# Sample attention of the second head pair beside the gates, its branch product at the end in full float32

## The chip, the core and the metric

The program runs on one core of a Trainium2 chip. The metric is the device time of one execution in microseconds (us), lower is better. Three runs of the kernel before gave 2956.97, 2960.16 and 2966.39 us; their median is 2960.16 us.

## What is computed

The reference is one layer of a hybrid decoder. It runs over 2048 prompt tokens and over 8 x 4 = 32 sample tokens, each with its own window of cached keys and values. Cut to what matters here:

```python
h = rms_norm(x, norm_pre_mix)
q, k, v, z1, z2, g_a, g_b = project_inputs(h, w_in, b_gate)     # gates: sigmoid(p + b_gate)
for gi, (win, dil) in enumerate(((128, 1), (512, 4), (2048, 16))):
    o, lse = dilated_group_prompt(...) or dilated_group_sample(...)   # 4 heads of 64 in each group
o_a = merge_dilations(outs, lses)                               # softmax over the three groups, 256 wide
o_b = z1 * (tril(w_spatial) @ layer_norm(z2) + b_spatial)       # 512 wide
merged = g_a * (o_a @ w_ao) + g_b * (o_b @ w_bo)                # 1024 wide
x = x + rms_norm(merged @ w_out, norm_post_mix)
x = x + rms_norm(square(relu(rms_norm(x, norm_pre_ffn) @ w_up)) @ w_down, norm_post_ffn)
```

For a sample token the attention of a group has 129 keys: rows of the cache at the group's dilation and the new rows of its own sequence. Everything is float32.

## The kernel before

The prompt is done in two halves of 1024 tokens (s = 0 and s = 1). The 32 sample tokens ride with the first half as columns 1024 to 1055 of every activation tile, so the first half has 1056 columns, in three chunks of 352. Each half goes through five stages: attention of the first pair of heads (hp = 0) over three groups, attention of the second pair (hp = 1), `gmlp`, `mix`, `out_rows`. After both halves comes the feed-forward part (`ffn`).

Most matrix products are done in a reduced float32 format (F32R) from split operands: a value is held as a high and a low part, and each product is three matmuls (high by high, high by low, low by high). `load_w` fetches a weight block over the SP queue (`raw`, two buffers), casts the high part on ScalarE (L264) and forms the low part on GpSimd (L267); `wh` and `wl` have two buffers each.

`mix` works on eight blocks of 128 channels. For each block it makes six gate products (two gates, three chunks, 8 K-tiles each, L283), applies the sigmoid on ScalarE (L1009), and then for each chunk makes the attention branch product `pa` (2 K-tiles from `oa`) and the gMLP branch product `pb` (4 K-tiles). VectorE multiplies the gates by them straight from PSUM (L1017 and L1019) and GpSimd adds the two (L1020). PSUM tiles of kind "g" have three buffers, of kind "s" two.

Work that is not a large product is written as Python generators in four lanes. A large product calls `tick` at certain K-tiles, and each tick takes one step of the first generator of each lane. That sets the order in which the program is written; a scheduling pass then sets the order on each engine's queue. Each engine runs its own queue strictly in order, and SP's queue issues nearly all transfers in order too.

`sample_attention(hp)` is one such generator, in lane 2. It does the attention of the sample tokens on VectorE, since the keys differ for each sequence: the 128 partitions hold 8 sequences by 16 key slots, and 30 steps take 4 keys' rows each. The score pass (L835 and L836, a product and a reduction for each of 30 steps) is followed by a softmax (L840 to L862, with two transposes on TensorE at L850 and L857), then the value pass (30 products L866, 14 pair sums L875 on VectorE, sums into `U` on GpSimd L876 and L878). Then one TensorE matmul sums over partitions (L882) and L894 transposes the result back into columns 1024 to 1055 of `oa`. The cache rows arrive in pieces of 256 KB (L807, L814, L817) in three buffers; one buffer holds the queries (L832).

Before, the generator of each head pair is pushed when that pair's first group has been projected, so that of hp = 1 runs beside the attention of hp = 1 and beside the first half of `gmlp`. There `drain(2)` makes it end before z1's second block is projected, since its buffers lie in `ov`, where z1 goes. `mix` drains lanes 0 to 2 in each block. The softmax merge of the three groups for the prompt tokens (`merge`, L751 to L766) runs at the same time in lane 1. `out_rows` multiplies by `w_out`; its own lane-2 work, `pre_mix_behind`, normalises the second half's inputs.

Of the kernel before, what the change touches and what calls it, by code (L numbers as in the profile page):

```python
# [10 lines left out]
F32 = mybir.dt.float32  # L11
# [7 lines left out]
P = 128  # L19
# [75 lines left out]
def hybrid_step(ctx: ExitStack, tc: tile.TileContext, ins: dict, outs: list):  # L95
# [176 lines left out]
    def gemm(w, offs, rhs, n, ticks=SLOW):  # L272

        calls[0] += len(offs) * n
        if calls[0] > SUM_EVERY:
            calls[0] -= SUM_EVERY
            step(3)
        pt = bank("g")
        last = len(offs) - 1
        for i, o in enumerate(offs):  # L280
            xh, xl = rhs(i)
            for j, (a, b) in enumerate(((w[0], xh), (w[0], xl), (w[1], xh))):
                nc.tensor.matmul(  # L283
                    pt[:, :n], a[:, o : o + P], b, start=(i == 0 and j == 0), stop=(i == last and j == 2)
                )
            tick(ticks.get(i, ()))
        return pt[:, :n]
# [489 lines left out]

    def sample_attention(hp):
        a0 = sm.tile([P, D], F32, tag="x", name="xt")
        a1 = sm.tile([P, D], F32, tag="x", name="xt")  # L780
        b0 = ov[:, A_X : A_X + 2048]
        q = a0[:, 0:512]
        U = a0[:, 512:1024]
        sc = a1[:, 0:240]
        pieces = [a1[:, 512:1024], b0[:, 0:512], b0[:, 512:1024]]
        prods = [b0[:, 1024:1536], b0[:, 1536:2048]]
# [100 lines left out]
        ot = sm.tile([8, 512], F32, tag="e0", name="sot")  # L887
# [9 lines left out]
        split(oh, ol, src, nc.vector)  # L897

# [94 lines left out]
    def mix(s):  # L993
        order = [4, 5, 6, 7, 0, 1, 2, 3]
        for m in range(8):
# [3 lines left out]
            gts = []  # L999
            for c, (c0, n) in enumerate(chunks(s)):  # L1000
                if c < 2:
                    gt = sm.tile([P, D], F32, tag="x", name="xt")
                else:
                    gt = sm.tile([P, D], F32, tag="t", bufs=1, name="junk")
                gts.append((gt[:, :512], gt[:, 512:]))
            for i, w in enumerate((wa, wb)):
                for c, (c0, n) in enumerate(chunks(s)):
                    pt = gemm(w, K8, act_rhs(c0, n), n)
                    nc.scalar.activation(  # L1009
                        gts[c][i][:, :n], pt, AF.Sigmoid, bias=b_gate[:, i * 8 + m : i * 8 + m + 1]  # L1010
                    )
            for lane in range(3):
                drain(lane)
            wo = load_w([w_ao[:, :, cs], w_bo[:, :, cs]])
            for (c0, n), (ga, gb) in zip(chunks(s), gts):
                pa = gemm(wo, K8[:2], lambda k: (oa[:, k, 0, c0 : c0 + n], oa[:, k, 1, c0 : c0 + n]), n)
                nc.vector.tensor_tensor(ga[:, :n], ga[:, :n], pa, ALU.mult)  # L1017
                pb = gemm(wo, K8[2:6], lambda k: (pair(k)[:, 0, c0 : c0 + n], pair(k)[:, 1, c0 : c0 + n]), n)
                nc.vector.tensor_tensor(gb[:, :n], gb[:, :n], pb, ALU.mult)  # L1019
                nc.gpsimd.tensor_tensor(row(order[m])[:, c0 : c0 + n], ga[:, :n], gb[:, :n], ALU.add)  # L1020
        for c0, n in chunks(s):
            for m in range(8):
                cc = slice(c0, c0 + n)
                split(act[:, m, 0, cc], act[:, m, 1, cc], row(order[m])[:, cc], nc.vector)

# [16 lines left out]
    def out_rows(s, behind=None):  # L1042
# [6 lines left out]
        if s == 0:  # L1049
            gain_next = gain_rows("norm_pre_mix", "t")  # L1050
            new_slot(3, False)
# [54 lines left out]
        if s == 0:  # L1106
            pt = gemm_rows([(list(zip(lhs(8), pa)), 256)], NSMP)
# [4 lines left out]
        if s == 0:  # L1112
            push(2, pre_mix_behind(1, gain_next, free))
# [400 lines left out]
    for s in range(2):  # L1514
# [6 lines left out]
        for hp in range(2):  # L1521
            for g in range(3):
# [66 lines left out]
```

## Time and profile before

| | |
|---|---|
| median of three runs | 2960.16 us |
| profiled execution, its own time | 2963.02 us |
| span of that execution in the trace | 2961.3 us |
| TensorE (PE) busy | 2849.7 us, 96% |
| VectorE (DVE) busy | 1307.1 us, 44% |
| ScalarE (ACT) busy | 1237.2 us, 42% |
| GpSimd (POOL) busy | 1192.5 us, 40% |

The 1.7 us between span and time lie outside the trace. The page cuts the span into 40 slices of 74 us and gives each engine's busy tenths in a digit. PEclk is TensorE's granted clock in tenths; it has two levels, 1.2 and 2.4 GHz, and a value between them is a mean over time at either. In a timeline row the bracket at the end says how long the engine stood idle before it and what ended the wait. In the first half, hp = 1 runs from about 296 us, `gmlp` reaches to about 497 us, the gates of `mix` follow, and `out_rows` starts at 758.8 us.

### The profile page before, as it was taken

The numbers are of one execution on the slowest core, as the hardware profiler recorded it, in microseconds if no ns is written. First come the engines' busy times: TensorE is split into PE (matmuls) and PEld (weight loads), VectorE is DVE, ScalarE is ACT, GpSimd is POOL, SyncE is SP. The second block draws the span as 40 slices with busy tenths as digits, with TensorE's granted clock in tenths as the row PEclk, the third lists the DMA queues.
The fourth block names the chain that finished last, engine by engine and source line by source line (L and its number), as shares of the span: only waits on it lengthen the run. The fifth ranks groups of instructions, "written<-read, shape, count | busy, mean of one in ns | idle before, by whom it ended". The sixth has DMA issues, their size and how long they took to land.

```text
span 2961.3 us, 44976 instructions
## 1 busy us (share of the span) xinstructions
PE 2849.7 (96%) x17350; PEld 2585.7 (87%) x17350; DVE 1307.1 (44%) x2284; ACT 1237.2 (42%) x2437; POOL 1192.5 (40%) x883
## 2 busy tenths in 40 slices
PE   7997998999998999999999999999999999999997
PEld 7897998999987887878889899999999888878885
DVE  5668687110463435450023654443333644452323
ACT  5353334212553433541135544554344555554343
POOL 3226234333312223143331344445555744445555
PEclk9998999999999999999999999999999999999998
DMA  5745654434459354253635887576665765586654
GB/s 164 189 117 158 192 145 132 111 96 109 143 177 238 122 146 116 80 135 83 150 92 198 297 270 246 181 247 207 201 205 192 238 206 185 192 275 191 191 182 149
DMA packets 463543, 514.45 MB, mean 174 GB/s; under 512 B 25440, under 2 KB 359840, under 8 KB 454112
## 3 DMA queue, kind: packets, MB, share of 16 engines
q1 hardware_dynamic: 452240, 474.54, 50.3%
q0 software_dynamic: 10944, 36.97, 6.9%
q8 instruction: 137, 2.24, 0.3%
q14 instruction: 78, 0.64, 0.1%
q10 hardware_dynamic: 144, 0.07, 0.0%
HBM read 395.92 MB, written 182.68 MB: 195 GB/s over the span
## 4 chain that ended last, share of the span: by engine, by line
PE 76%; DMA 10%; DVE 8%; POOL 2%; issue 2%; ACT 1%; SPq 0%; DVEq 0%; POOLq 0%; ACTq 0%
PE pg L283 25%; PE pd L1288 19%; PE pe L1288 10%; PE pe L1368 10%; PE pg L297 6%; DMA xt<-h 2%; PE pu L694 2%; DMA junk<-us 2%; DMA h<-h 1%; DMA us<-ov 1%; PE pt L680 1%; DMA hd<-xt 1%; DVE ov L835 1%; DMA xt<-smp 1%; DVE xt L866 1%
## 5 line engine op out<-in xcount | busy, mean ns | idle before, releaser
L283 PE MATMUL pg<-act,wh 128*128 128x352 f32 (+3 forms) x3424 | 951.4, 356 | 8.5 <-ACT ov L989 4.9
L1199 POOL TENSOR_TENSOR wf<-raw,wf 128x512 fp32r<-128x512 f32 x448 | 635.1, 1420 | 686.2 <-ACT wf L1198 630.7
L283 PEld LDWEIGHTS pg<-act,wh 128*128 128x128 f32 x3424 | 620.5, 192 | 61.3 <-ACT ov L989 5.2
L283 PE MATMUL pg<-act,wl 128*128 128x352 f32 (+3 forms) x1712 | 607.2, 355 | 0.0
L1198 ACT CAST wf<-raw 128x512 fp32r<-128x512 f32 x448 | 277.2, 619 | 502.0 <-PE pd L1288 190.7
L267 POOL TENSOR_TENSOR wl<-raw,wh 128x1024 fp32r<-128x1024 f32 (+1 forms) x106 | 254.5, 2402 | 360.8 <-ACT wh L264 337.1
L1288 PE MATMUL pd<-act,wf 128*128 128x264 f32 x2880 | 361.9, 285 | 8.6 <-ACT act L1198 5.2
L1288 PEld LDWEIGHTS pd<-act,wf 128*128 128x128 f32 x2880 | 355.2, 189 | 9.8 <-ACT act L1198 5.4
L283 PEld LDWEIGHTS pg<-act,wl 128*128 128x128 f32 x1712 | 328.4, 192 | 26.8
L1368 PE MATMUL pe<-wf,act 128*128 128x512 f32 x1008 | 237.6, 396 | 4.8 <-POOL wf L1199 4.1
L1368 PEld LDWEIGHTS pe<-wf,act 128*128 128x128 f32 x1008 | 190.2, 189 | 50.9 <-POOL wf L1199 5.4
L264 ACT CAST wh<-raw 128x1024 fp32r<-128x1024 f32 (+1 forms) x104 | 105.3, 1012 | 254.0 <-PE pg L283 141.6
L1297 DVE TENSOR_TENSOR ov<-pd,ov 128x528 f32<-128x528 f32 x140 | 96.2, 704 | 204.8 <-PE pd L1288 204.3
L1288 PE MATMUL pd<-pair,wf 128*128 128x264 f32 x1440 | 184.7, 284 | 0.0
L1288 PE MATMUL pe<-act,wf 128*128 128x512 f32 x768 | 182.6, 392 | 0.1
L1288 PEld LDWEIGHTS pd<-pair,wf 128*128 128x128 f32 x1440 | 178.2, 188 | 0.0
L1199 DVE TENSOR_TENSOR act<-flat,act 128x1024 fp32r<-128x1024 f32 (+1 forms) x76 | 103.1, 1359 | 157.4 <-ACT act L1198 157.2
L1288 PEld LDWEIGHTS pe<-act,wf 128*128 128x128 f32 x768 | 143.8, 188 | 32.9 <-ACT pair L1198 0.3
L652 ACT ACTIVATE ov<-ov 128x256 f32<-128x256 f32 (+1 forms) x192 | 91.8, 478 | 186.7 <-DVE ov L648 185.4
L1017 DVE TENSOR_TENSOR xt<-xt,pg 128x352 f32<-128x352 f32 (+1 forms) x32 | 19.3, 604 | 300.8 <-PE pg L283 164.0
L1297 DVE TENSOR_TENSOR ov<-pe,ov 128x512 f32<-128x512 f32 x136 | 91.5, 687 | 137.2 <-PE pe L1288 126.3
L1288 PE MATMUL pd<-oa,wf 128*128 128x264 f32 x1056 | 135.0, 284 | 0.0
(254 smaller groups left out, 4263.8 us busy)
## 6 DMA issues: line engine op xcount, KB each, us to landing
raw<-in_w_in_dram SPq DMA_DIRECT2D x84, 512.0 KB
raw<-up_sums SPq DMA_DIRECT2D x128, 256.0 KB
raw<-down_sums SPq DMA_DIRECT2D x128, 256.0 KB
flat<-f SPq DMA_DIRECT2D x48, 528.0 KB
raw<-in_w_up_dram SPq DMA_DIRECT2D x96, 256.0 KB
raw<-in_w_down_dram SPq DMA_DIRECT2D x96, 256.0 KB
flat<-f SPq DMA_DIRECT2D x48, 512.0 KB
f<-ov SPq DMA_DIRECT2D x16, 1056.0 KB
```

The lines of the kernel that those rows point to most:

```text
L264: nc.scalar.copy(wh[:, :o], raw[:, :o])
L267: eng.tensor_tensor(wl[:, :o], raw[:, :o], wh[:, :o].bitcast(F32), ALU.subtract)
L283: nc.tensor.matmul(pt[:, :n], a[:, o : o + P], b, start=(i == 0 and j == 0), stop=(i == last and j == 2))
L297: nc.tensor.matmul(pt[:n, o : o + width], a, b, start=(i == 0 and j == 0), stop=(i == last and j == 2))
L652: nc.scalar.activation(pb[:, h, :w], pb[:, h, :w], AF.Exp, scale=-1.0, bias=uo[:, u, 128 + h : 129 + h], accum_out=uo[:, u, 130 + h : 131 ...
L680: nc.tensor.transpose(pt[:, h, e * P : (e + 1) * P], pb[:, h, e * P : (e + 1) * P], ident)
L694: nc.tensor.matmul(up[:, hs], tb[:, h, e * P : (e + 1) * P], vv[:, hs], start=(e == 0), stop=(e == len(rows) - 1),)
L1198: nc.scalar.copy(high, raw)
L1199: eng.tensor_tensor(low, raw, high.bitcast(F32), ALU.subtract)
L1288: nc.tensor.matmul(pt[:, o : o + n], w[:, a], x[:, b, c : c + n], start=first and j == 0, stop=last and j == 2)
L1297: nc.vector.tensor_tensor(X[to], res, X[add], ALU.add)
L1368: nc.tensor.matmul(pts[t], x[k][:, c, t * P : (t + 1) * P], w[:, d, 0], start=k == 0 and j == 0, stop=k == 15 and j == 2)
```

## The change

Sample attention of hp = 0 stays where it was. That of hp = 1 is pushed in `mix`, after the gate products of the first channel block. It gets other buffers there: two pieces in place of three, and products, queries, sums and scores in tiles of their own. The attention branch product `pa` leaves the sample columns out and its PSUM tiles are of kind "s". The gates of the sample columns (`ga`, and `gb` already multiplied by the gMLP branch) are copied aside by ScalarE. A new generator `sample_branch`, pushed at the end of `mix`, fetches `w_ao` once more, multiplies it in full float32 with the sum of the two parts of `oa`, and makes the sample columns of the merged activation; `out_rows` drains lane 2 before its ninth block of rows, which is the sample tokens. The gate tiles now hold all chunks of one gate each, in place of both gates of one chunk, in both halves. The lanes are drained in the first block only. The gain rows for the second half's norm use the tile in which the gates were kept, so they are fetched after that drain.

```diff
-    def gemm(w, offs, rhs, n, ticks=SLOW):
+    def gemm(w, offs, rhs, n, ticks=SLOW, kind="g"):
...
-        pt = bank("g")
+        pt = bank(kind)
...
     def sample_attention(hp):
+        if hp == 0:
...
+            pieces = [a1[:, 512:1024], b0[:, 0:512], b0[:, 512:1024]]
+            prods = [b0[:, 1024:1536], b0[:, 1536:2048]]
+        else:
+            a0 = sm.tile([P, D], F32, tag="gbc", bufs=1, name="gbc")
+            q = late["t"][:, 0:512]
+            U = sm.tile([P, 512], F32, tag="o4", bufs=1, name="o4")
+            sc = sm.tile([P, 512], F32, tag="zs", bufs=1, name="zs")[:, :240]
+            pieces = [a0[:, 0:512], a0[:, 512:1024]]
+            prods = [sm.tile([P, 512], F32, tag="e0", name="prod") for _ in range(2)]
...
+    def sample_branch():
+
+        smp2 = late["t"][:, 512:].rearrange("p (i m t) -> p i m t", i=2, m=8)
+        tt = slice(HALF, TMAX)
+        wk = []
+        for k in range(2):
+            t = sm.tile([P, D], F32, tag="x", name="xt")
+            nc.sync.dma_start(t, w_ao[:, k])
+            wk.append(t)
+        yield
+        o = sm.tile([P, 3, NSMP], F32, tag="smp", name="smp")[:, :2]
+        nc.vector.tensor_tensor(o, oa[:, :, 0, tt].bitcast(F32), oa[:, :, 1, tt].bitcast(F32), ALU.add)
+        yield
+        yield
+        pt = ps.tile([P, 512], F32, tag="t", name="pt")[:, : 8 * NSMP].rearrange("p (m t) -> p m t", m=8)
+        for m in range(8):
+            for k in range(2):
+                nc.tensor.matmul(pt[:, m], wk[k][:, m * P : (m + 1) * P], o[:, k], start=k == 0, stop=k == 1)
+        nc.vector.tensor_tensor(smp2[:, 0], smp2[:, 0], pt, ALU.mult)
+        nc.vector.tensor_tensor(smp2[:, 0], smp2[:, 0], smp2[:, 1], ALU.add)
+        split(act[:, :, 0, tt], act[:, :, 1, tt], smp2[:, 0], nc.vector)
+        yield
...
     def mix(s):
...
-            for lane in range(3):
-                drain(lane)
+            if m == 0:
+                for lane in range(3):
+                    drain(lane)
+                if s == 0:
+                    push(2, sample_attention(1))
             wo = load_w([w_ao[:, :, cs], w_bo[:, :, cs]])
...
+            for c0, n in chunks(s):
+                na = min(n, HALF - c0)
+                aa, bb = slice(c0, c0 + na), slice(c0, c0 + n)
+                pa = gemm(wo, K8[:2], lambda k: (oa[:, k, 0, aa], oa[:, k, 1, aa]), na, kind="s")
+                nc.vector.tensor_tensor(ga[:, aa], ga[:, aa], pa, ALU.mult)
+                pb = gemm(wo, K8[2:6], lambda k: (pair(k)[:, 0, bb], pair(k)[:, 1, bb]), n)
+                nc.vector.tensor_tensor(gb[:, bb], gb[:, bb], pb, ALU.mult)
+                nc.gpsimd.tensor_tensor(row(order[m])[:, aa], ga[:, aa], gb[:, aa], ALU.add)
+            if s == 0:
+                for i, gt in enumerate((ga, gb)):
+                    nc.scalar.copy(smp2[:, i, m, :], gt[:, HALF:])
...
+        if s == 0:
+            push(2, sample_branch())
...
         if s == 0:
-            gain_next = gain_rows("norm_pre_mix", "t")
             new_slot(3, False)
...
         if s == 0:
+            drain(2)
             pt = gemm_rows([(list(zip(lhs(8), pa)), 256)], NSMP)
             copy_any(of(8)[0][:, :256], pt)
...
         if s == 0:
+            gain_next = gain_rows("norm_pre_mix", "t")
             push(2, pre_mix_behind(1, gain_next, free))
...
-                    if g == 0:
-                        push(2, sample_attention(hp))
+                    if g == 0 and hp == 0:
+                        push(2, sample_attention(0))
```

The scheduling pass moves whole queues with this. On VectorE, around the gate products of the fourth channel block of the first half, there stand in the kernel before only those products (L1017 by `pa`, L1019 by `pb`; `xt` and `junk` are the gate tiles, `pg` is PSUM):

```order
L1017 TENSOR_TENSOR xt<-xt,pg 128x352
L1019 TENSOR_TENSOR xt<-xt,pg 128x352
L1017 TENSOR_TENSOR xt<-xt,pg 128x352
L1019 TENSOR_TENSOR xt<-xt,pg 128x352
L1017 TENSOR_TENSOR junk<-junk,pg 128x352
L1019 TENSOR_TENSOR junk<-junk,pg 128x352
```

At the same place of the changed kernel they are L1053 and L1055, and L877 and L886 are the value products and pair sums of sample attention (`gbc` holds the cache pieces, `zs` the weights of the softmax, `prod` and `junk` products):

```order
L877 TENSOR_TENSOR junk<-gbc,zs 128x512
L877 TENSOR_TENSOR prod<-gbc,zs 128x512
L886 TENSOR_TENSOR prod<-prod,junk 128x512
L1053 TENSOR_TENSOR xt<-xt,ps 128x352
L877 TENSOR_TENSOR junk<-gbc,zs 128x512
L877 TENSOR_TENSOR prod<-gbc,zs 128x512
L1055 TENSOR_TENSOR xt<-xt,pg 128x352
L886 TENSOR_TENSOR prod<-prod,junk 128x512
```

Sixteen of the 30 value products stand ahead of that block's first L1053, six stand among its six gate products, eight behind them. On TensorE's queue the matmul that sums `U` over partitions, L882 before, stood among projection matmuls of `gmlp` (`pg_4686` is one such product):

```order
L283 MATMUL pg_4686<-act_75,wh_4681 128x352 x2
L283 MATMUL pg_4686<-act_75,wl_4682 128x352
L882 MATMUL pt_4183<-xt_2845,con_78 8x512
L283 MATMUL pg_4686<-act_75,wh_4681 128x352 x2
L283 MATMUL pg_4686<-act_75,wl_4682 128x352
```

In the changed kernel it is L893 and stands near the end of the fifth gate product of the fifth channel block (`pg_6055`; the sixth is `pg_6081`), while the second transpose of the softmax, L868, stands near the end of the fourth block's first gate product:

```order
L283 MATMUL pg_6055<-act_75,wl_5930 128x352
L893 MATMUL pt_5972<-o4_4929,con_78 8x512
L283 MATMUL pg_6055<-act_75,wh_5929 128x352 x2
L283 MATMUL pg_6055<-act_75,wl_5930 128x352
L283 MATMUL pg_6081<-act_75,wh_5929 128x352 x2
```

On SP's queue, where the weights of the fourth and fifth blocks followed one another, cache pieces (`gbc`) now stand between them (`raw` are the weights):

```order
L248 DMA raw<-in_w_in_dram 128x8x128
L828 DMA gbc<-smp_104 128x1x512
L825 DMA gbc<-in_cache_kv_w_dram 128x4x128
L248 DMA raw<-in_w_in_dram 128x8x128
L825 DMA gbc<-in_cache_kv_w_dram 128x4x128 x6
L828 DMA gbc<-smp_106 128x1x512
L825 DMA gbc<-in_cache_kv_w_dram 128x4x128
L248 DMA raw<-in_w_ao_dram 128x2x128
```

Each piece here goes into one of two buffers, so its transfer stands on SP until the product that read that buffer is done. From the end of `mix` of the first half on, the queues keep the order that they had.

## Rows read from the trace of the kernel before

**Rows 1.** The page: TensorE's busy time, and the busy tenths of TensorE and VectorE in 40 slices.

```profile
PE 2849.7 (96%) x17350; PEld 2585.7 (87%) x17350; DVE 1307.1 (44%) x2284; ACT 1237.2 (42%) x2437; POOL 1192.5 (40%) x883
...
PE   7997998999998999999999999999999999999997
...
DVE  5668687110463435450023654443333644452323
```

**Rows 2.** Busy time by stretch: the stretch and its length, busy us (and instructions) of TensorE, its weight loads, VectorE, ScalarE and GpSimd, then TensorE's granted clock, the DMA share and GB/s. The first stretch is hp = 1 and `gmlp` of the first half, the second `mix`, the third both attentions and `gmlp` of the second half.

```profile
296.00:518.00 222.00, 200.72 (x1265) 194.76 (x1266) 170.12 (x367) 88.68 (x200) 83.65 (x73) 0.93 0.56 156
518.00:757.00 239.00, 238.76 (x1486) 237.94 (x1485) 41.84 (x80) 57.03 (x94) 81.67 (x58) 1.00 0.39 103
...
960.00:1330.00 370.00, 358.58 (x2008) 305.86 (x2008) 173.24 (x469) 160.56 (x386) 110.69 (x117) 0.99 0.45 120
```

**Rows 3.** TensorE's timeline of the first stretch: start, duration, the instruction, and the idle time ahead of it with what ended it. These are all waits over 0.3 us there.

```profile
331.23 0.33 PE L646 MATMUL ps<-pair,oa 128*128 128x128 f32 x1 [1.32 <-DVE ov L648]
...
342.58 0.33 PE L646 MATMUL ps<-pair,oa 128*128 128x128 f32 x1 [2.22 <-DVE ov L648]
357.58 0.87 PE L283 MATMUL pg<-act,wh 128*128 128x352 f32 x2 [1.77 <-DVE pair L515]
...
378.50 0.47 PE L646 MATMUL ps<-pair,oa 128*128 128x128 f32 x1 [5.68 <-DVE ov L648]
...
453.00 0.75 PE L283 MATMUL pg<-act,wh 128*128 128x352 f32 x2 [4.93 <-ACT ov L989]
...
465.31 1.88 PE L882 MATMUL pt<-xt,con 128*8 128x512 f32 x2 [5.19 <-POOL xt L878]
```

**Rows 4.** Stretches at or behind four of these waits, with the columns of rows 2.

```profile
340.00:350.00 10.00, 7.78 (x44) 7.45 (x43) 6.33 (x20) 4.39 (x15) 0.40 (x1) 0.83 0.70 204
...
370.00:380.00 10.00, 4.32 (x26) 4.03 (x26) 1.38 (x7) 1.50 (x6) 0.40 (x1) 0.74 0.92 234
...
453.00:456.40 3.40, 3.40 (x12) 3.40 (x13) 3.40 (x3) 3.36 (x5) 3.40 (x2) 0.54 0.41 117
...
465.30:470.00 4.70, 4.69 (x12) 2.98 (x13) 2.89 (x9) 2.99 (x5) 2.19 (x2) 0.50 0.26 78
```

**Rows 5.** VectorE's timeline ahead of the waits at 331, 342 and 378 us.

```profile
328.49 0.69 DVE L835 TENSOR_TENSOR ov<-xt 128x512 f32<-128x512 f32 x1 [4.49 <-DMA xt<-smp]
...
341.62 0.69 DVE L835 TENSOR_TENSOR ov<-xt 128x512 f32<-128x512 f32 x1 [2.71 <-DMA xt<-in_cache_kv_w_dram]
...
378.14 0.29 DVE L648 CUSTOM_DVE_ANT_0 ov<-ps,con 128x128 f32<-128x128 f32 x1 [8.46 <-DMA us<-ov]
```

**Rows 6.** ScalarE's timeline ahead of the wait at 453 us.

```profile
450.03 0.21 ACT L754 ACTIVATE e<-e 128x6 f32<-128x6 f32 x1 [12.02 <-DVE e L753]
```

**Rows 7.** VectorE's groups from 408 to 463 us, the value pass of hp = 1: operation, tiles and shapes, count, busy us, mean ns, idle ahead.

```profile
L875 DVE TENSOR_TENSOR ov<-ov,xt 128x512 f32<-128x512 f32 x14 | 11.7, 832 | 0.2
L866 DVE TENSOR_TENSOR xt<-ov,xt 128x512 f32<-128x512 f32 x10 | 11.3, 1133 | 1.3 <-DMA ov<-in_cache_kv_w_dram 1.2
L866 DVE TENSOR_TENSOR ov<-ov,xt 128x512 f32<-128x512 f32 x10 | 9.1, 914 | 1.1 <-POOL xt L876 1.1
...
L866 DVE TENSOR_TENSOR ov<-xt 128x512 f32<-128x512 f32 x5 | 5.6, 1119 | 0.0
L866 DVE TENSOR_TENSOR xt<-xt 128x512 f32<-128x512 f32 x5 | 4.2, 847 | 0.1
```

**Rows 8.** SP's queue: the issue of a cache piece, and that of the gain rows at the start of `out_rows`.

```profile
427.14 0.38 SPq L814 DMA_DIRECT2D ov<-in_cache_kv_w_dram  x1
...
762.64 0.33 SPq L399 DMA_DIRECT2D gbc<-in_norm_pre_mix_dram  x1
```

**Rows 9.** VectorE's timeline: the first value product, the one that waited for the piece of rows 8, the first gate products of the second and third block of `mix`, the first use of the gain rows, and the split of the first block normalised with them.

```profile
407.79 0.69 DVE L866 TENSOR_TENSOR xt<-xt 128x512 f32<-128x512 f32 x1
...
430.20 0.78 DVE L866 TENSOR_TENSOR xt<-ov,xt 128x512 f32<-128x512 f32 x1 [1.06 <-DMA ov<-in_cache_kv_w_dram]
...
559.83 0.52 DVE L1017 TENSOR_TENSOR xt<-xt,pg 128x352 f32<-128x352 f32 x1 [23.75 <-PE pg L283]
...
591.75 0.52 DVE L1017 TENSOR_TENSOR xt<-xt,pg 128x352 f32<-128x352 f32 x1 [23.32 <-PE pg L283]
...
767.17 4.06 DVE L368 SCALAR_TENSOR_TENSOR xt<-xt,rs,gbc 128x1024 f32<-128x1024 f32 x2 [1.44 <-DMA gbc<-in_norm_pre_mix_dram]
...
797.70 0.69 DVE L311 TENSOR_TENSOR act<-pt,act 128x512 fp32r<-128x512 f32 x1
```

**Rows 10.** GpSimd's timeline: the last sum of the value pass, and the last sum of `mix`.

```profile
464.00 1.25 POOL L878 TENSOR_TENSOR xt<-xt,ov 128x512 f32<-128x512 f32 x1
...
761.67 0.94 POOL L1020 TENSOR_TENSOR ov<-junk 128x352 f32<-128x352 f32 x1 [0.90 <-DVE junk L1019]
```

**Rows 11.** Who waited for whom on TensorE up to 900 us: total us, times, longest; the two waits at the sum over partitions.

```profile
PE pt L882 <- DVE el L756: 6.5, 1, 6.5
...
PE pt L882 <- POOL xt L878: 5.2, 1, 5.2
```

**Rows 12.** TensorE's groups from 500 to 800 us in full float32: the 32 gMLP matmuls of `w_tril` and the 4 of `w_bd`, with two records for each.

```profile
L954 PE MATMUL pt<-w_tril,ov 128*128 128x128 f32 x64 | 9.1, 274 | 0.0
...
L961 PE MATMUL pt<-w_bd,zs 32*128 32x32 f32 x8 | 1.6, 282 | 0.0
```

**Rows 13.** The longest wait of TensorE at the end of `gmlp` of the second half, which has no sample attention.

```profile
1294.19 1.16 PE L954 MATMUL pt<-w_tril,ov 128*128 128x128 f32 x8 [2.25 <-DVE gtmp L965]
```

More of the change, by code (lines that the diff above doesn't have):

```diff
@@ L775, in merge @@
             yield
+    late = {}
     def sample_attention(hp):
[L779 to L786, printed above, removed]
+        if hp == 0:
+            a0 = sm.tile([P, D], F32, tag="x", name="xt")
+            a1 = sm.tile([P, D], F32, tag="x", name="xt")
+            b0 = ov[:, A_X : A_X + 2048]
+            q = a0[:, 0:512]
+            U = a0[:, 512:1024]
+            sc = a1[:, 0:240]
+            pieces = [a1[:, 512:1024], b0[:, 0:512], b0[:, 512:1024]]
[7 more added lines that the diff above has]
+            prods = [sm.tile([P, 512], F32, tag="e0", name="prod") for _ in range(2)]
         cnt = [0, 0]
@@ L886, in sample_attention @@
         nc.vector.reciprocal(rl, pl[:8, :8])
-        ot = sm.tile([8, 512], F32, tag="e0", name="sot")
+        ot = prods[0][:8, :] if hp else sm.tile([8, 512], F32, tag="e0", name="sot")
         nc.vector.tensor_tensor(
@@ L994, in mix @@
         order = [4, 5, 6, 7, 0, 1, 2, 3]
+        if s == 0:
+            late["t"] = sm.tile([P, D], F32, tag="t", bufs=1, name="junk")
+            smp2 = late["t"][:, 512:].rearrange("p (i m t) -> p i m t", i=2, m=8)
         for m in range(8):
@@ L998, in mix @@
             wb = load_w([w_in[:, :, 4352 + m * P : 4352 + (m + 1) * P]])
[L999 to L1007, printed above, removed]
+            ga, gb = (sm.tile([P, TMAX], F32, tag="x", name="xt") for _ in range(2))
@@ L1008, in mix @@
+            for i, (w, gt) in enumerate(((wa, ga), (wb, gb))):
+                for c0, n in chunks(s):
                     pt = gemm(w, K8, act_rhs(c0, n), n)
                     nc.scalar.activation(
-                        gts[c][i][:, :n], pt, AF.Sigmoid, bias=b_gate[:, i * 8 + m : i * 8 + m + 1]
+                        gt[:, c0 : c0 + n], pt, AF.Sigmoid, bias=b_gate[:, i * 8 + m : i * 8 + m + 1]
                     )
-            for lane in range(3):
-                drain(lane)
-            wo = load_w([w_ao[:, :, cs], w_bo[:, :, cs]])
@@ L1015, in mix @@
[L1015 to L1020, printed above, removed]
+            if m == 0:
[3 more added lines that the diff above has]
+                    push(2, sample_attention(1))
@@ new lines, in mix @@
+            wo = load_w([w_ao[:, :, cs], w_bo[:, :, cs]])
+            for c0, n in chunks(s):
+                na = min(n, HALF - c0)
[5 more added lines that the diff above has]
+                nc.gpsimd.tensor_tensor(row(order[m])[:, aa], ga[:, aa], gb[:, aa], ALU.add)
```

3 lines of the change are left out of this document (2 added, 1 removed).

## The prediction

> **What bounds the kernel now.** I read the page first: TensorE is busy for 96% of the span [rows 1], so time is won only where it stands idle or runs at the lower clock, and lost wherever a new wait is put on its queue. The slices show where that is. VectorE's digits are 5 to 8 in the first seven slices, where TensorE has two 7s and an 8, and 1, 1, 0 in the three after them, where TensorE has 9s. Next the stretches [rows 2]: hp = 1 and `gmlp` leave TensorE idle for 222.0 - 200.7 = 21.3 us at a mean clock of 0.93, while `mix` is full (238.76 of 239 us, clock 1.00) with VectorE busy for 42 us. The change carries VectorE work from the first into the second: 11.3 + 9.1 + 5.6 + 4.2 + 11.7 = 41.9 us of the value pass [rows 7], and a score pass of 30 products and 30 reductions, about as much again. Last, TensorE's own timeline says which waits make up the 21 us: six, together 21.1 us [rows 3].
>
> **What goes.** Two waits for scores lie behind sample products: VectorE stood 4.49 us and 2.71 us for a sample piece, and the mask step that TensorE needed was queued behind it [rows 5]. The wait at 453 us is ScalarE's: its queue stood 12.02 us at an exponential of the prompt's merge, whose input came late from a VectorE full of value products [rows 6]. The wait at 465 us is the sum over partitions itself. Together 1.32 + 2.22 + 4.93 + 5.19 = 13.7 us.
>
> Behind three of them the clock fell to the lower level [rows 4]: a mean of 0.83 over 10 us is 3.4 us at half speed, worth 1.7 us; then 0.54 over 3.4 us, worth 1.6; and 0.50 over 4.7 us, worth 2.3. That is 5.6 us, so 19.3 us in all.
>
> I do not count the other two waits. The one at 357 us hung on a key split with no sample operation at work, and the one at 378 us on the write of `us`, for which VectorE stood 8.46 us [rows 5]. Their idle time is 7.4 us [rows 3], and the clock of the second is worth about 2.6 us by its mean of 0.74 over 10 us [rows 4]. If both went too, the gain would be 10 us larger.
>
> Without sample work this stretch becomes like its twin in the second half, which loses 11.4 us over both head pairs and `gmlp` [rows 2]. Its waits behind the merge and the gMLP gates, the longest 2.25 us [rows 13], have no counterpart in the first half before, since the sample waits came there instead. I add 3 us for them, one such wait and a little, between 0 and 5 for two.
>
> **What is added on TensorE.** `sample_branch` makes 16 full-float32 matmuls. A full-float32 matmul leaves two records: 64 for the 32 of `w_tril`, at 9.1/64 = 0.14 us each, and 8 for the four small ones, at 1.6/8 = 0.20 [rows 12]. So 32 records cost 4.5 to 6.4 us; I take 4.5, the row with the same weights' shape. The Trainium skill, "FP8 and Floating Point Precision", section "TensorE Precision Notes", counts four passes through the array for true float32. The records show two; by four of the same length the price would be 9 us, and the sum 4.5 us higher.
>
> Saved are 32 columns of 8 x 6 matmuls. A block of `mix` takes 591.75 - 559.83 = 31.9 us [rows 9] for 22 K-tiles x 3 matmuls x 1056 columns, or 0.46 ns a column, so 1536 columns are 0.7 us. The sample attention's own matmuls are as many as before; they only move.
>
> **What is put in the way in `mix`.** The gate products are hidden work for VectorE, and the 80 to 90 us fit into idle time. But TensorE's queue now holds five matmuls that wait for the sample chain, and behind each the gate products of the prompt are queued. The tightest is L893, which needs the finished `U`. By its place it comes 4.8 gate products into the fifth block; a gate product of 8 x 3 x 352 columns takes 3.9 us, so 18.6 us after that block starts. The transpose that opens the value pass comes 3.9 us into the fourth block, and the first product follows it after a few short steps, say at 5 us. That leaves 31.9 - 5 + 18.6 = 45.5 us.
>
> The pass needs its 41.9 us of products and pair sums, six gate products of 0.52 us [rows 9] and a last sum of 1.25 us on GpSimd [rows 10]: 46.2 us with no wait for data. Now the data: a piece issued at 427.14 us was used at 430.20 us [rows 8, 9], 3.1 us later. With two buffers, two products take at least 3.1 + 1.0 = 4.1 us, or 2.0 each, against 41.9/30 = 1.4 us that VectorE needs for each. Eighteen of the 30 products have a piece of their own, so this adds up to 11 us, and nothing if pieces land in 1.8 us, as a lighter loaded queue may allow. I take 5 us. TensorE then waits 46.2 + 5 - 45.5, about 6 us, near to the 6.5 and 5.2 us that it waited at the same matmul before [rows 11]. A wait of that size was followed by about 2 us of lost clock [rows 4]. So 8 us, with bounds of 0 and 14.
>
> The Trainium skill, "DMA: Bandwidth & Descriptors", section "Anatomy of one DMA — SWDGE (gpsimd) path", fits a transfer that GpSimd issues by 2.0 us plus its bytes at 436 GB/s, hence 2.6 us for 256 KB as an estimate. By that, two products take 3.6 us, the 18 lose 7 us in place of 5, and the sum is 2 us higher. It speaks against a ring of two; the row at 3.1 us, under load, does so more.
>
> The score pass has more room: 30 steps from the first block's gates to the end of the third block. There only the gate products queued behind the steps can suffer, and PSUM's two and three buffers give TensorE about 4 us. I cost that at nothing. If the 2.0 us per step held throughout, 13 steps would stand in one block of 31.9 us; the cover would just be used up.
>
> **The end of `mix`.** The two fetches of `w_ao` wait for the gate tiles, free at 761.67 + 0.94 = 762.6 us in the old times [rows 10]. A 512 KB load issued at that moment was first used 4.5 us later [rows 8, 9], so the matmuls could start at about 767 us. They stand some 8 us behind the start of `out_rows` at 758.8 us, so they are about on time; I add 1 us, between 0 and 3. The gain rows are fetched some 10 us later than before. Before, they were used at 767.2 us and the first block that they serve was split into place at 797.7 us [rows 9], so 30 us of row products cover the delay; without that cover it would be the 10 us. The coarser gate tiles let the next block's sigmoid start only after the last sum of the block, 1 to 2 us behind the last product; a gate product of 3.9 us covers it.
>
> **Sum.** -19.3 + 3 + 4.5 - 0.7 + 8 + 1 = -3.5 us. From the profiled execution, 2963.0 us, that gives 2959.5; its time is 2.9 us above the median of the runs, so against the median I forecast 2956.7, say 2957 us. A measurement of this kernel can tell about 0.3%, or 9 us, from no change, so this reads as the same. Its own range, with the bounds of the terms, is 2948 to 2965.
>
> **Rivals.**
>
> *The chain keeps pace.* Pieces land in under 2 us, VectorE's products take 0.7 us as the one of rows 9 does, and L893 finds its sum ready. Then the 8 us fall away, and one or both of the uncounted waits (up to 10 us) may go, since the queues of that stretch are dealt anew. That is 2949 to 2939, say 2942 us. For it: VectorE is idle for more than 80% of `mix` [rows 2]. Against it: before, at the same place of the same chain, TensorE waited both times [rows 11].
>
> *The ring of two starves.* The price is the same 0.6 us per piece and more, but in both passes, because transfers of weights and of the `up` sums share the queue and SP holds weights behind waiting pieces. VectorE then brings the gate products late and TensorE waits at PSUM in several blocks as well as at L893. With 11 us in each pass and 4 us of clock, the 8 us become 26 and the time 2975 us. It decides from a landing time of about 5 us per piece, against the 3.1 us measured [rows 8, 9]. For it: three buffers before, two now. Against it: the score pass has slack of whole blocks.
>
> *The change does not bring what it takes away for.* The waits of hp = 1 return in other places, set by the writes of `us` (5.7 us there already, with VectorE empty) and by the merge, and only the last two waits go. The gain is 9 us in place of 19 and the time about 2967 us.
>
> **How the numbers follow.** The forecast has 0.43, of which 0.06 lies below 2951; the chain that keeps pace 0.30; the starved ring 0.17; the last rival 0.10, half of it within 9 us. So faster 0.36, the same 0.42, slower 0.22. The range of 2938 to 2974 takes in the first rival, the third and most of the second.
>
> **What would show it.** Right: no wait of TensorE at the sum over partitions or behind ScalarE between 440 and 470 us, a wait of 3 to 10 us at L893 in the fifth block of `mix`, the wait for `us` near 378 us still there, and 32 records of L927 at 0.14 us. Wrong: a `mix` without idle time (then the first rival), waits at `ps` or `pg` in several blocks with VectorE idle behind cache pieces (the second), or new waits of 5 us in hp = 1 (the third).

## The result, and the profile after

| | median us | range us | ratio to the kernel before |
|---|---|---|---|
| before, beside it | 2964.94 | 2956.97 to 2971.22 | |
| changed | 2970.81 | 2965.84 to 2975.26 | 1.0019 (95% interval 1.0011 to 1.0027) |

The changed kernel is 5.9 us slower, 0.19%. The profiled execution took 2969.44 us, its span 2967.7. The page answers to [rows 1]: VectorE's digits of slices five to seven have fallen from 6, 8, 7 to 4, 5, 6, and those of eight and nine risen from 1, 1 to 4, 6.

```profile
PE 2854.4 (96%) x17382; PEld 2588.2 (87%) x17382; DVE 1323.3 (45%) x2288; ACT 1243.7 (42%) x2457; POOL 1185.7 (40%) x883
...
PE   8997999889998999999999999999999999999997
...
DVE  5668456460473435451023654353343644452323
```

The stretches, cut at about the same places of the program as in [rows 2]: hp = 1 with `gmlp`, then `mix`.

```profile
296.00:492.00 196.00, 191.20 (x1257) 187.72 (x1258) 97.97 (x266) 87.27 (x198) 59.39 (x60) 0.97 0.41 109
492.00:760.00 268.00, 246.24 (x1486) 241.87 (x1485) 120.63 (x177) 62.59 (x110) 100.11 (x66) 0.96 0.51 139
```

The first stretch is 26 us shorter; the second, full before, now leaves TensorE idle for 21.8 us. TensorE's waits of over 0.5 us in the changed kernel, from hp = 1 up to the start of `out_rows`:

```profile
412.52 0.66 PE L948 MATMUL pt<-con,flat 128*128 128x128 f32 x4 [0.62 <-ACT ov L949]
418.38 0.28 PE L955 MATMUL pt<-con,flat 128*32 128x128 f32 x1 [1.45 <-ACT ov L949]
429.61 0.66 PE L772 MATMUL pt<-con,o 128*128 128x128 f32 x2 [2.59 <-ACT ov L949]
...
517.33 0.59 PE L283 MATMUL pg<-act,wh 128*128 128x352 f32 x2 [1.23 <-DVE xt L1055]
548.95 0.90 PE L283 MATMUL ps<-oa,wh 128*128 128x320 f32 x2 [10.05 <-DVE xt L1053]
618.71 0.56 PE L283 MATMUL ps<-oa,wh 128*128 128x320 f32 x2 [2.65 <-DVE xt L1053]
...
650.80 1.88 PE L893 MATMUL pt<-o,con 128*8 128x512 f32 x2 [7.64 <-POOL o L889]
768.28 0.38 PE L297 MATMUL pg<-wl,act 128*128 128x256 f32 x1 [1.22 <-POOL wl L267]
```

All six waits of [rows 3] are gone, the two that I had not counted among them. The last row stood at 764.99 us before: by then the kernel is 3.3 us behind. The first gate product tells how far ahead it had been, first before, then after:

```profile
527.10 0.51 DVE L1017 TENSOR_TENSOR xt<-xt,pg 128x352 f32<-128x352 f32 x1
```

```profile
500.80 0.52 DVE L1053 TENSOR_TENSOR xt<-xt,ps 128x352 f32<-128x352 f32 x1 [0.42 <-PE ps L283]
```

So 26.3 us are won ahead of the gate products and 29.6 lost in `mix`. VectorE's timeline ahead of the longest wait shows where:

```profile
538.07 1.29 DVE L846 TENSOR_TENSOR prod<-junk,gbc 128x512 f32<-128x512 f32 x2 [3.69 <-DMA junk<-smp]
539.28 1.27 DVE L847 TENSOR_REDUCE zs<-prod 128x8 f32<-128x512 f32 x2
543.28 3.99 DVE L846 TENSOR_TENSOR prod<-junk,gbc 128x512 f32<-128x512 f32 x2 [2.73 <-DMA gbc<-in_cache_kv_w_dram]
547.20 1.27 DVE L847 TENSOR_REDUCE zs<-prod 128x8 f32<-128x512 f32 x2
548.39 0.50 DVE L1053 TENSOR_TENSOR xt<-xt,ps 128x352 f32<-128x352 f32 x1
```

The gate product at 548.39 had its PSUM bank full long before: TensorE had stood since 538.9 us. It stood in VectorE's queue behind score products, one of which waited 3.69 us for the next group's query and one 2.73 us for a cache piece. Another 2.7 us came from the two products at 543.28, which took 3.99 us where the two at 538.07 took 1.29: GpSimd formed the low part of a weight from 543.51 to 546.11 us, and the experiments on the running sums show what that does to VectorE. The score pass as a whole (480 to 565 us; count, busy us, mean ns, then the idle time ahead by what ended it):

```profile
L846 DVE TENSOR_TENSOR prod<-junk,gbc 128x512 f32<-128x512 f32 x30 | 29.8, 1016 | 24.5 <-DMA gbc<-in_cache_kv_w_dram 13.1 <-DMA junk<-smp 8.8 <-DMA gbc<-smp 2.3
L847 DVE TENSOR_REDUCE zs<-prod 128x8 f32<-128x512 f32 x30 | 19.4, 676 | 0.1
```

SP's own waits there (engine, line, what it waited for: total us, times, longest) show why the pieces were late. They are not issued until products have freed their buffers, and in order:

```profile
SPq L825 <- DVE prod L846: 19.4, 10, 4.7
SPq L828 <- DVE zs L847: 10.5, 1, 10.5
```

### The profile page after: what moved, and what is told of

Its sections match the earlier page's. It is cut to its first block, busy times and chain, and to the rows that moved or that the text cites. A ratio compares the mean times of both kernels' runs of the same rounds, so it can differ in the third digit from the quotient of the medians.

```text
span 2967.7 us, 45073 instructions
## 1 busy us (share of the span) xinstructions
PE 2854.4 (96%) x17382; PEld 2588.2 (87%) x17382; DVE 1323.3 (45%) x2288; ACT 1243.7 (42%) x2457; POOL 1185.7 (40%) x883
## 5 line engine op out<-in xcount | busy, mean ns | idle before, releaser
L1330 PEld LDWEIGHTS pd<-oa,wf 128*128 128x128 f32 x1056 | 130.9, 188 | 0.4 <-DVE oa L1241 0.3
```

What stands on the lines that cost most here:

```text
L1330: nc.tensor.matmul(pt[:, o : o + n], w[:, a], x[:, b, c : c + n], start=first and j == 0, stop=last and j == 2)
```

## The experiments

Each difference below is the median against that of the kernel before on the same chip, with the ratio's 95% interval.

**Pieces and queries, each alone and together.** Six pieces:

```diff
             pieces = [a0[:, 0:512], a0[:, 512:1024]]
+            pieces += [row(i)[:, o : o + 512] for i in (2, 3) for o in (0, 512)]
```

> Only the ring of key and value pieces grows for the second pair: six buffers instead of two (the four new ones are halves of two rows of ov that stand empty until the seventh gate block). The changed kernel is 5.9 us above the kernel before. Theory (the ring of two starves the score pass, and the gate products stand behind its waits in DVE's queue): the waits of 1.23, 10.05 and 2.65 us on a gate product go, and the half-speed stretches of 13.7 and 3.4 us with them, 17 to 19 us in all; the time is 11 to 13 us under the kernel before, and DVE's idle time ahead of L846 for cache pieces falls from 13.1 us to under 4. Rival (the query that is loaded again into the one buffer at each group sets the waits, 8.8 us of DVE's idle time): the piece waits fall, but the wait of the second block stays above 4 us and the time is 0 to 5 us above the kernel before. Second rival (SP's queue is held by weight loads, so that more buffers bring no earlier issue): nothing moves, 4 to 7 us above.

Measured: +2.5 us (0.9996 to 1.0015). Piece waits fell from 13.1 us to 0.3, but the first rival was right as well. With the pieces on time the query was late, at 529.23 us, and the gate product of the second block stood behind it. VectorE's and TensorE's timelines:

```profile
529.23 1.29 DVE L847 TENSOR_TENSOR prod<-junk,gbc 128x512 f32<-128x512 f32 x2 [7.76 <-DMA junk<-smp]
```

```profile
544.79 0.90 PE L283 MATMUL ps<-oa,wh 128*128 128x320 f32 x2 [7.02 <-DVE xt L1054]
618.26 0.90 PE L283 MATMUL ps<-oa,wh 128*128 128x320 f32 x2 [6.62 <-DVE xt L1054]
```

Queries ahead, with two pieces as in the change:

```diff
+        qs = [q] * 3 if hp == 0 else [q, row(1)[:, 0:512], row(1)[:, 512:1024]]
...
+        if hp:
+            for g in range(3):
+                nc.sync.dma_start(qs[g], smp_d[g][hp][0].unsqueeze(1).to_broadcast([8, 16, 512]))
...
-            nc.vector.tensor_tensor(t4(pr), t4(q), rows, ALU.mult)
+            nc.vector.tensor_tensor(t4(pr), t4(qs[g]), rows, ALU.mult)
```

> Only the queries of the second pair change: the three groups get a buffer each (two in a row of ov that stands empty) and are all issued ahead of the first piece; the ring keeps two pieces. Theory (ring of two): DVE's waits of 5.11 and 3.69 us on a query go, the piece waits stay; of the 10.05 us on a gate product 3 to 4 go, 4 to 5 us with the clock; the time is 0 to 3 us above the kernel before. Rival (the query reload): the 10.05 us go to under 3 and the time is 6 to 9 us under the kernel before.

Measured: +5.2 us (1.0009 to 1.0032), no gain at all; even the 3 to 4 us of the theory did not come. The queries' 8.8 us went over to the pieces, 13.1 to 22.3 us. TensorE's wait is the same 10.07 us at 547.27.

```profile
L851 DVE TENSOR_TENSOR prod<-ov,gbc 128x512 f32<-128x512 f32 x18 | 17.6, 985 | 23.2 <-DMA gbc<-in_cache_kv_w_dram 22.3 <-DMA gbc<-smp 0.9
```

> Six pieces and three query buffers together. Theory (both only feed the same waits of DVE's queue): all TensorE waits on L1053 and L1055 are under 1 us, 17 to 21 us less than the changed kernel, 11 to 15 us under the kernel before; the wait of 7.6 us ahead of L893 stays. Rival (DVE's own work, 53 us in 67 us of the score pass, is what holds the products): waits of 2 to 5 us on L1053 stay in the second block with every piece landed in time, and the time is 0 to 6 us under the kernel before.

Measured: -6.1 us (0.9967 to 0.9992), 12 us less than the changed kernel, below the 17 to 21 expected. The second block's wait on a gate product is gone, so pieces and queries were two limits, one behind the other. The fourth block's has grown from 2.65 to 6.62 us, as it had with six pieces alone; this is the value pass, and neither theory had it there. The scheduling pass has a part in it, since each edit changes its order as well. Ahead of the fourth block's first gate product on VectorE stand 17 value products and 8 pair sums in the changed kernel (the sixteen given with the change leave out one), 20 and 9 in the two runs with six pieces. Ahead of the second block's stand 25 of the 30 score products in the changed kernel and all 30 in these two runs. What the buffers did and what the order did was not run apart.

```profile
542.23 0.43 PE L283 MATMUL pg<-act,wl 128*128 128x352 f32 x1 [0.82 <-POOL wl L267]
610.08 0.90 PE L283 MATMUL ps<-oa,wh 128*128 128x320 f32 x2 [6.62 <-DVE xt L1059]
632.50 1.87 PE L899 MATMUL pt<-o,con 128*8 128x512 f32 x2 [3.45 <-POOL o L895]
```

**The running sums.** In the value pass of this run VectorE hardly waits for data, yet products of 0.68 us take 1.78. The changed kernel shows it best, VectorE first, then GpSimd:

```profile
599.71 0.68 DVE L877 TENSOR_TENSOR prod<-gbc,zs 128x512 f32<-128x512 f32 x1
600.31 1.78 DVE L877 TENSOR_TENSOR junk<-gbc,zs 128x512 f32<-128x512 f32 x1
602.13 2.23 DVE L886 TENSOR_TENSOR prod<-prod,junk 128x512 f32<-128x512 f32 x1
```

```profile
599.94 1.61 POOL L887 TENSOR_TENSOR o<-o,prod 128x512 f32<-128x512 f32 x1 [1.42 <-DVE prod L886]
601.50 2.30 POOL L267 TENSOR_TENSOR wl<-raw,wh 128x768 fp32r<-128x768 f32 x1
```

The second product ends at 602.09, 0.54 us behind the end of GpSimd's sum (601.55); the pair sum at 604.36, 0.56 behind the end of GpSimd's weight split (603.80). It looks as if VectorE stood still while GpSimd ran and then did its work. The Trainium skill, "SBUF — State Buffer", section "Who interferes with whom", states such a lock for a VectorE instruction with two SBUF inputs against a GpSimd instruction that reads SBUF, and none for a reduction; the trace agrees, with the reductions of L847 between 668 and 691 ns, whatever GpSimd did, beside products at 1016 on average. So the sum was moved, on top of pieces and queries:

```diff
-                nc.gpsimd.tensor_tensor(U, U, pair_sum, ALU.add)
+                (nc.vector if hp else nc.gpsimd).tensor_tensor(U, U, pair_sum, ALU.add)
```

> The run with six pieces and three query buffers, and the running sum of the value pass (L887) on DVE instead of GpSimd. In that run a product beside GpSimd's sum took 1.78 us and one by itself 0.68, and TensorE waited 6.62 us on a gate product in the fourth block. Theory (DVE and GpSimd slow each other on these tiles, 1.10 us for each of 15 sums, and a sum on DVE takes 0.69): the products keep 0.7 us, DVE is done with the value pass some 6 to 10 us earlier, the waits of 6.62 and 3.45 us shrink to under 4 us together, and the time is 10 to 17 us under the kernel before. Rival (the value pass is bound by its pieces or by DVE's count of instructions): the sums add 10 us to DVE, the wait of the fourth block grows past 8 us, and the time is 0 to 5 us under the kernel before.

Measured: -22.9 us (0.9914 to 0.9943), more than expected, and 16.8 us less than the run before it. In the two traces the stretch from the first pair's sum over partitions to the start of `out_rows` goes from 464.7 to 450.6 us. Nothing over 0.5 us is left in `mix` but the wait at the closing sum, 1.80 us; the products take 682 to 833 ns:

```profile
L893 DVE TENSOR_TENSOR o<-o,prod 128x512 f32<-128x512 f32 x14 | 15.3, 1090 | 0.3
L892 DVE TENSOR_TENSOR prod<-prod,junk 128x512 f32<-128x512 f32 x14 | 11.0, 786 | 0.0
L883 DVE TENSOR_TENSOR junk<-ov,zs 128x512 f32<-128x512 f32 x11 | 9.2, 833 | 0.0
L883 DVE TENSOR_TENSOR prod<-ov,zs 128x512 f32<-128x512 f32 x12 | 8.2, 682 | 0.0
```

In the run before, products of the same shapes took 1038 and 1470 ns and pair sums 1080. With 15.3 us of sums added, VectorE's value pass is 2 us shorter, 48.4 for 50.7 us. The order moved here too: ahead of the fourth block's first gate product stand 16 products, 7 pair sums and 6 sums, in place of 20 products and 9 pair sums. That is 29 instructions in both runs, and VectorE came through them in 19.9 instead of 30.9 us. But the order may have a share: in the run before, 17 products and 8 pair sums were done 5.5 us ahead of the gate product, and TensorE's wait there was 6.62 us. That the products are shortened by taking the sums off GpSimd is shown; how much of the time came by that and how much by the new order is not.

The same edit alone, on the changed kernel:

> The changed kernel with one edit: the second pair's running sum (L887) on DVE; two pieces and one query buffer as in the change. Theory (the score pass is held by pieces and queries, the value pass by DVE beside GpSimd's sums): the wait of 10.05 us in the second block stays, the waits of 2.65 and 7.64 us of the value pass shrink by half or more; 4 to 9 us less than the changed kernel, 3 us under to 2 us above the kernel before. Rival (the value pass at two pieces is bound by its pieces, 7 us of DVE's idle time): no gain, 4 to 8 us above the kernel before.

Measured: +2.1 us (0.9993 to 1.0016), 3.8 us less than the changed kernel, just outside the theory on both counts. The fourth block's wait went; the second block's stayed, and so, against the theory, did that at L893. There VectorE's value pass stood idle for 8.0 us behind pieces, so with two pieces the chain is late by its data, as the rival had it, though not its 4 to 8 us above.

```profile
548.37 0.90 PE L283 MATMUL ps<-oa,wh 128*128 128x320 f32 x2 [10.59 <-DVE xt L1053]
646.03 1.86 PE L893 MATMUL pt<-o,con 128*8 128x512 f32 x2 [8.14 <-DVE o L889]
```

And on the kernel before, for both pairs:

> The kernel before with one edit: the running sums of the value pass of both pairs on DVE instead of GpSimd. It tells how much of the 22.9 us of the run with pieces, queries and sums belongs to the move of the second pair. Theory (the move brings the larger part: its waits in the attention and gMLP stage came from DVE's load there, of which the sums are a small part): 0 to 8 us under the kernel before, with waits of over 10 us together still between 330 and 470 us. Rival (the sums are all of it): 14 to 23 us under.

Measured: -4.3 us (0.9972 to 0.9991). The sums are a small part; the kernel before keeps waits of 3.13 us at 336 and 8.89 us at 464, among others. The rest of the 22.9 us needs the move.

> The run with pieces, queries and sums on DVE, and the first pair's sums on DVE as well. Theory (GpSimd's sums stretch DVE's products of the first pair by some 0.4 us each net, in a stage where DVE holds TensorE): 0 to 6 us less than that run, 23 to 29 us under the kernel before. Rival (the first pair's products are not on the path): the same within 3 us.

Measured: -23.5 us (0.9905 to 0.9934), 0.6 us less than without, which lies inside both ranges, so the run does not decide between them. In its trace the wait of 4.78 us at the first pair's sum over partitions is gone, but waits of 2.63 us at 368 and 2.55 us at 419 are new, and `out_rows` starts at 744.76 us where it started at 744.80.

**The closing sum later.**

```diff
-        yield
-        yield
+        for _ in range(16 if hp else 2):
+            yield
         pu = ps.tile([P, 512], F32, tag="t", name="pt")
```

With eight steps:

> Only the closing sum of the second pair moves: its matmul (L893) is issued eight steps behind the last value product instead of two, some 11 us later. Theory: the wait of 7.64 us and the half-speed stretch of 6.8 us that follows go, 9 to 11 us; the time is 3 to 5 us under the kernel before, and the 10.05 us in the second block stay. Rival (the wait is only moved on, since the sample branch ends later and out_rows waits for it): the gain is under 4 us, with a new wait of over 3 us at the start of out_rows or ahead of L927.

Measured: +6.5 us (1.0010 to 1.0033). This tested nothing: the program's scheduler had L893 at row 2410 of TensorE's order and put it at 2409, and TensorE waited 7.91 us there. With sixteen:

> As the run with eight steps, with sixteen: there the matmul L893 kept its place among TensorE's instructions (row 2409 for 2410) and its wait (7.91 us); here it stands 65 rows, some 15 us of gate matmuls, further back. Theory (the chain ends a few us after its own matmul, so a later matmul finds the sum ready): the wait of 7.6 us is under 1 us and the half-speed stretch after it goes, 8 to 10 us in all; the time is 2 to 5 us under the kernel before. Rival (the sample branch is then late at out_rows): a new wait of over 3 us ahead of L927 or at the start of out_rows, and the time 1 to 5 us above the kernel before.

Measured: +2.5 us (0.9998 to 1.0023), 3.4 us less than the changed kernel. The wait at L893 went, but its rival came in another place than I named, waits on the low part of a weight. TensorE, then GpSimd:

```profile
648.87 0.43 PE L283 MATMUL ps<-oa,wl 128*128 128x352 f32 x1 [1.87 <-POOL wl L267]
662.25 0.43 PE L283 MATMUL pg<-act,wl 128*128 128x352 f32 x1 [2.97 <-POOL wl L267]
```

```profile
645.77 1.28 POOL L887 TENSOR_TENSOR o<-o,prod 128x512 f32<-128x512 f32 x1 [3.31 <-DVE prod L886]
647.00 1.81 POOL L267 TENSOR_TENSOR wl<-raw,wh 128x768 fp32r<-128x768 f32 x1
```

A sum that waits for VectorE holds the weight split queued behind it on GpSimd. The second wait, at 662 us, was not followed up. On top of the other three edits:

> The run with pieces, queries and sums on DVE, and the closing matmul sixteen steps behind the last value product, as in the run that did this alone. Theory (only its 1.80 us wait is left there): 0 to 2 us less than without, 21 to 26 us under the kernel before. Rival (the later branch of the sample tokens, or a weight's low part on GpSimd, waits instead, as in the run that did this alone): 1 to 4 us more, with a wait on wl L267 in the gate stage.

Measured: -22.6 us (0.9905 to 0.9932), as without it. The wait of 1.80 us is gone, but so small a gain does not show in the time.

**The move and the end, apart.**

```diff
-                    push(2, sample_attention(1))
+                    for a in range(2):
+                        nc.vector.tensor_copy(oa[:, 1, a, HALF:TMAX], oa[:, 0, a, HALF:TMAX])
```

> The attention of the sample tokens' second pair of heads is left out altogether: its output columns are copied from the first pair's. The gates, the merge order and the float32 branch at the end stay as in the changed kernel. Theory (attention and gMLP gained 26 us, and the second pair's score and value passes in the gate stage gave it back: 21.8 us of TensorE waits and some 7 us of half clock): the gate stage shows no TensorE wait over 1 us, and the time is 19 to 25 us under the kernel before. Rival (the other edits give it back: the gate tiles, the fp32 matmuls, the later gain load): the time is 0 to 10 us under the kernel before.

Measured: -24.0 us (0.9910 to 0.9934). `mix` is full, and at full clock:

```profile
488.00:728.00 240.00, 240.00 (x1496) 240.00 (x1496) 34.76 (x69) 57.08 (x105) 76.60 (x53) 1.00 0.40 109
```

The other way round, the second pair beside the attention again and only the end changed:

```diff
-        if hp == 0:
+        if hp < 2:
...
-                if s == 0:
-                    push(2, sample_attention(1))
...
-                    if g == 0 and hp == 0:
-                        push(2, sample_attention(0))
+                    if g == 0:
+                        push(2, sample_attention(hp))
```

> The second pair runs beside the attention as in the kernel before, with that kernel's buffers; the gate tiles, the one drain of the merge and the float32 branch at the end stay as in the changed kernel. Theory (the branch costs 4.3 us of fp32 matmuls, 1 to 2 us of half clock after them, less 0.6 us of columns, and the gates nothing): the waits of the second attention stage are back, the gate stage has none over 1 us, and the time is 3 to 8 us above the kernel before. Rival (the merge and the gMLP gates, no longer drained at the same places, let the attention stage wait less even so): 0 to 10 us under the kernel before. Rival (the gates' own order costs): over 10 us above.

Measured: +2.8 us (0.9997 to 1.0019), just under the theory's 3 to 8. The waits of [rows 3] are back, and the start of `out_rows` stands where it stood before:

```profile
379.47 0.47 PE L646 MATMUL ps<-pair,oa 128*128 128x128 f32 x1 [5.60 <-DVE ov L648]
...
454.51 0.95 PE L283 MATMUL pg<-act,wh 128*128 128x352 f32 x2 [4.89 <-ACT ov L1023]
467.36 1.88 PE L893 MATMUL pt<-xt,con 128*8 128x512 f32 x2 [5.89 <-POOL xt L889]
765.23 0.38 PE L297 MATMUL pg<-wl,act 128*128 128x256 f32 x1 [1.22 <-POOL wl L267]
```

So the second pair costs 2.8 + 24.0 = 26.8 us beside the attention, 5.9 + 24.0 = 29.9 beside the gates as the change puts it, and 24.0 - 22.9 = 1.1 with pieces, queries and sums mended. The last is less than the runs can tell, some 4 us to each side. By the traces it is 3.9 us from the first pair's sum to the start of `out_rows` (450.6 and 446.7 us), and 3.0 of them are the pair's own matmuls (below).

## Why the prediction was wrong

The time, 2970.8 us, lies inside the range of 2938 to 2974, but the change went the other way: 3.5 us less was forecast, and it is 5.9 more. Of the 13.8 us between 2957 and 2970.8, 4.8 are the kernel before itself, 2964.94 us beside the changed kernel and 2960.16 when I forecast. The forecast's own range was too narrow for its terms, too: their bounds add up to -15.5 to +8.4 us, or 2945 to 2969, not 2948 to 2965. Term by term:

- *What goes.* -19.3 + 3 was too small: 26.3 us were won by the first gate product. I had left out the waits at 357 and 378 us, the second because its cause looked like the write of `us`. Both went, and the run with the end alone brought both back (1.76 and 5.60 us), so the second pair decides them. They were worth 10.3 us, 7.4 idle and, in slices of 5 us, 1.3 and 1.6 of clock; for the second I had read 2.6, over 10 us of which TensorE worked 4.3. The waits that I added came too, 0.62 + 1.45 + 2.59 = 4.7 us, and with them a cost that I had not added: behind the last of them TensorE worked 6.39 us at a mean clock of 0.53, another 3.0 us (first row below), so 7.7 against 0 to 5. Two gains stood in no term. The wait at the first pair's sum over partitions fell from 6.51 to 4.79 us, and the second pair's own matmuls left this stretch for `mix`, 0.27 + 0.22 + 0.20 + 1.88 + 0.41 = 3.0 us. So -19.3 + 7.7 - 10.3 - 1.7 - 3.0 = -26.6, near the 26.3. That the difference is about the "10 us larger" that I named is in part luck.
- *L893.* 8 us were forecast, 6 idle and 2 of clock. It waited 7.64 us, and the clock behind it was at half speed for most of 3.6 us (fourth row; the rows are stretches with the columns of [rows 2]):

```profile
429.00:436.00 7.00, 6.39 (x24) 6.42 (x25) 7.00 (x15) 1.90 (x4) 3.11 (x2) 0.53 0.25 72
...
541.80:555.50 13.70, 6.55 (x24) 6.55 (x25) 9.56 (x13) 1.05 (x1) 4.20 (x4) 0.52 0.83 198
...
620.00:624.00 4.00, 3.80 (x15) 3.35 (x14) 2.47 (x5) 0.95 (x1) 2.94 (x2) 0.59 0.26 77
650.80:654.40 3.60, 3.60 (x9) 1.90 (x10) 0.68 (x1) 0.51 (x1) 0.00 (x0) 0.56 0.98 258
776.00:781.00 5.00, 5.00 (x31) 5.00 (x31) 3.13 (x3) 2.07 (x3) 2.75 (x2) 0.66 0.70 230
```

  The fourth row gives 3.6 x 0.44 = 1.6 us, so the term is 9.2.
- *The step that failed* is "The score pass has more room … I cost that at nothing". It cost 1.23 + 10.05 us of waiting and, by the second row above, 6.55 x 0.48 = 3.1 us of clock: 14.4 us. The room was there, since VectorE was through with the score pass at 565 us and then idle for 13.84 us. But room at the end of a chain does not help work queued in its middle: an in-order queue hands each of its waits to whatever stands behind. I had worked out 2.0 us per step from the piece that took 3.1 us; the 30 steps took 29.8 + 19.4 + 24.5 us, 2.5 each, and the idle part of it in lumps of up to 6.3 us, some close together, where I had put PSUM's cover at about 4. A part of it is neither room nor data: 29.8 us for 30 products are 0.99 each, where one by itself takes 0.68, and the longest stand beside GpSimd's weight splits. The query, loaded into one buffer anew for each group, was in no step of mine, and the two runs with one edit each show that either limit alone is enough.
- *The value pass* was priced at L893 alone. In the fourth block it also held a gate product: 2.65 us and, by the third row, 4 x 0.41 = 1.6 us of clock. Its row means above 0.69 us stood in [rows 7]; 41.9 us over 44 instructions are 0.95 each. I took that for VectorE's own need. With the sums on VectorE, in the kernel before, the same 44 take 35.0 us, so 6.9 us of the 41.9 went with GpSimd's sums; that the rest above 0.69 each comes from its weight splits is likely, but not shown.
- *The end.* The 32 records of L927 begin between 771.8 and 776.1 us, but eight matmuls of `out_rows` stand among them. Without those they hold TensorE from 771.81 to 771.96 and from 772.99 to 776.26 us, 3.4 in all and 0.11 each, where I forecast 4.5 and 0.14. They are two records a matmul, where the Trainium skill, "FP8 and Floating Point Precision", section "TensorE Precision Notes", counts four passes. With the end alone, the split of [rows 9] at 797.70 stands at 801.48: 3.8 us, of which 0.2 were there before, so about the price of the matmuls. In the changed kernel it stands at 806.10, 8.4 us late, 5.1 since the start of `out_rows`. The 1.5 us more are about the clock's, which stood in no term: in the 5 us behind L927 its mean was 0.66 (last row above), worth 1.7 us, and with the end alone it was 1.00. Why it fell in one and not in the other is open. About 2 us of that are won back at the start of the second half, where a wait of 4.64 us at 918.69 becomes 1.79.

Summed, -26.3 + 14.4 + 4.2 + 9.2 - 0.7 (columns) = +0.8 us at the start of `out_rows`, where 3.3 were measured. The second pair's own matmuls, which moved into `mix` with it and stand in no term, are 3.0 us more by their records: 3.8 us. From the measured 3.3, +5.1 and -2 give the +6.4 us of the spans.

Of the rivals, the ring that starves came nearest, 2975 us with waits at PSUM in several blocks beside L893, and I gave it 0.17. The chain that keeps pace describes the kernel with three more edits: 22.9 us under the kernel before, where that rival said 18.

## What to carry to other kernels

When work is moved under a stage that looks idle on an engine, ask not whether the engine has time but what stands behind each of the moved instructions in its queue, and how long the longest single wait is against the buffers that cover it. A chain fed by small buffers needs all its feeds ahead (here pieces and queries) before any shows a gain, so mend them together before judging the move. And read an instruction's time beside what the neighbour engine ran at that moment: the running sum moved from GpSimd to VectorE, where it adds work, took the time from 6.1 to 22.9 us under the kernel before with pieces and queries mended, and from 5.9 to 2.1 us above it without. Look at the queues' order as well: an edit that goes through a scheduling pass can change it far from its own lines.

## What was not expected of the hardware

- GpSimd's 1.6 us sum stretched a VectorE product from 0.68 to 1.78 us, and its weight split a pair sum to 2.23, each ending about 0.55 us behind GpSimd's instruction; reductions took 668 to 691 ns throughout.
- Two waits in series hid each other: query waits of 8.8 us, taken away, came back as 9.2 us of piece waits, to the same wait of TensorE (10.05 and 10.07 us).
- A matmul written six steps later in the program kept its place in TensorE's order (row 2409 for 2410). The written order was not the queue's.
